# First feed-forward of a two-layer diffusion step: some lo parts of the weights by accumulating on-chip transfers, four more adaLN units on VectorE

## The chip, the cores and the metric

The kernel runs on one core of one Trainium2 chip. The time is microseconds of that core for one execution; the median of three runs counts. Profile times are microseconds from the start of the profiled execution's span, unless marked ns. Engines: PE is TensorE's matmul and PEld its weight load, DVE is VectorE, ACT ScalarE, POOL GpSimd, SP the engine that issues the loads.

## The reference, cut to what matters

Two token groups of 128 (context and latents) go through two layers. Every layer has a mixer and a gated feed-forward, each with a shift, a scale and a gate from the conditioning vector (adaLN):

```python
mod = jax.nn.silu(cond) @ w_ada[l] + b_ada[l]
sh1, sc1, gt1, sh2, sc2, gt2 = jnp.split(mod[:, None, :], 6, axis=-1)
h = rmsnorm(x, g_norm_mix[l]) * (1 + sc1) + sh1
...
x = x + gt1 * m
h = rmsnorm(x, g_norm_ffn[l]) * (1 + sc2) + sh2
x = x + gt2 * conv_ffn(h, w_ffn_up[l], w_ffn_conv[l], b_ffn_conv[l], w_ffn_down[l])
```

`conv_ffn` multiplies by `w_up` (2048 x 11264), convolves over three positions, multiplies the silu of one half by the other and multiplies by `w_down` (5632 x 2048). Everything is float32. Layer 0 has latent and grouped-query attention, layer 1 differential attention.

## The kernel before, in words

**Products.** A float32 product is made of three passes: each operand is split into hi, rounded to the matmul's type, and lo = raw - hi, and hi x hi, hi x lo and lo x hi are added in PSUM. Weights come as raw tiles of 1 MB (128 partitions x 16 blocks of 128; three buffers `raw`). `Weights.chunk` splits a tile in two halves of eight blocks: ScalarE casts raw to `wh`, VectorE subtracts to `wl` (`split`, L248 and L249; four buffers of each). `gemm` then runs 16 blocks (22 for `w_down`) x 3 matmuls of 128 x 256. Where `Weights.ahead` splits (the first products of a stage, pinned), `chunk` does not.

**adaLN units.** One unit (layer, j of six, quarter q) is 512 columns of `w_ada`, four tiles of 1 MB. It is made in one of two ways. On TensorE (`ROWS`): 16 matmuls of 32 x 512 in two pairs of steps, a copy, four transposes and a reduction (`sum_rows`, `ada_finish`); in the mixer of layer 1 these stand within the products. On VectorE (`FEATS`): eight multiply-and-sum instructions of 128 x 2048, two to a tile (`feature_step`, L473, out `junk`), two buffers `araw`, and a small add (L479). `RLIMIT` and `FLIMIT` are how far each list may be worked off by the end of a stage.

**What sets the order.** The program is written stage by stage; a scheduler puts each engine's instructions in order, save those marked to keep the written order (`keep_order`, `between`, the sums of `feature_step`). In a feed-forward, `pump(0, rate)` follows each product and hands out sums at `FRATE`: 0.7 after each of the 82 products of `up` past the first three pairs, 1.42 after 28 of the 32 of `down`. Whatever is left up to `FLIMIT` is done by a loop at the end of `ffn`. Behind the first feed-forward comes `modulated` for layer 1: its first three products (of `w_in_c`) run on the unnormed rows `u`; within the first, after 6 of 16 blocks, TensorE sums the squares (`stats`), VectorE and GpSimd make the factor (`rv` L219, `rr` L222), and after 13 blocks TensorE spreads it (`factor`). These products are pinned. The rows of the normed operand (L799 to L811) follow on VectorE, ScalarE and GpSimd.

**Queues.** All loads go through SP's queue in one order; GpSimd issues none.

Of the kernel before, what the change touches and what calls it, by code (L numbers as in the profile page):

```python
# [11 lines left out]
F32 = mybir.dt.float32  # L12
F32R = mybir.dt.float32r
AF = mybir.ActivationFunctionType
ALU = mybir.AluOpType
# [3 lines left out]
P = 128  # L19
# [57 lines left out]
ROWS = [(0, j, q) for q in range(4) for j in (1, 0)]  # L77
ROWS += [(0, j, q) for j in (2, 4) for q in range(4)]
ROWS += [(0, 5, 0)]
ROWS += [(1, 2, 1), (1, 2, 2), (1, 2, 3), (1, 4, 0), (1, 3, 0)]  # L80
FEATS = [(0, 5, 1), (0, 5, 2), (0, 5, 3)]
FEATS += [(1, j, q) for j in (1, 0) for q in range(4)]
FEATS += [(1, 2, 0)]
FEATS += [(1, 5, q) for q in range(4)]
DEEP = [[(0, 3, q) for q in range(4)], [(1, 4, q) for q in range(1, 4)] + [(1, 3, q) for q in range(1, 4)]]
RLIMIT = {"ab": 16, "ffn0": 17, "c": 22, "ffn1": 22}
FLIMIT = {"ab": 0, "ffn0": 12, "c": 12, "ffn1": 16}

SIDE = {"in3": 0.4, "heads": 1.6, "out0": 1.8, "c": 2.2, "outc": 2.0}
UW = NT + 2  # L90
# [4 lines left out]
def step_kernel(ctx: ExitStack, tc: tile.TileContext, A: dict):  # L95
    nc = tc.nc
    dve, act, pool, sp = nc.vector, nc.scalar, nc.gpsimd, nc.sync
# [25 lines left out]
    wpool = ctx.enter_context(tc.tile_pool(name="wpool", bufs=3))  # L123
# [8 lines left out]
    def banks(name):  # L132
        return tc.tile_pool(name=name, bufs=1, space=PSUM)
# [3 lines left out]
    def nm(s):  # L137
        uid[0] += 1
        return f"{s}_{uid[0]}"

    def T_(pl, shape, tag, dt=F32, bufs=None):
        kw = {} if bufs is None else {"bufs": bufs}
        return pl.tile(shape, dt, tag=tag, name=nm(tag), **kw)
# [39 lines left out]
    def step():  # L183
        for g in list(chains):
            if next(g, chains) is chains:
                chains.remove(g)
# [60 lines left out]
    def split(out_hi, out_lo, src, pin=lambda i: i):  # L247
        pin(act.copy(out_hi, src))  # L248
        pin(dve.tensor_tensor(out=out_lo, in0=src, in1=out_hi.bitcast(F32), op=ALU.subtract))  # L249
# [3 lines left out]
    class Weights:  # L253
# [3 lines left out]
        def __init__(self, src, nblk, per_tile, cycle=0):  # L257
            self.src, self.nblk, self.per = src, nblk, per_tile
            self.cycle = cycle
            self.at, self.blocks, self.tiles = 0, [], []  # L260
            self.half = None
            self.begun = []
            self.used = lambda: None

        def load(self, parts=1, pin=lambda i: i):
            n = self.per
            if self.cycle:
                n = min(n, self.cycle - self.at * n % (-(-self.cycle // n) * n))
            n *= self.nblk if self.per < TB else 1
            raw = T_(wpool, [P, 4, 512], "raw").rearrange("p g n -> p (g n)")  # L270
            w = n * P // parts
            for i in range(parts):
                s = slice(i * w, (i + 1) * w)
                pin(sp.dma_start(out=raw[:, s], in_=self.src[self.at, :, s]))
            self.at += 1
            return raw, n

# [26 lines left out]
        def chunk(self):  # L304
            while len(self.blocks) < self.nblk:
                if self.half:
                    self.ahead(lambda i: i)
                    continue
                raw, n = self.take()
                n0 = FINE if fine[0] else 8  # L310
                for lo in range(0, n, n0):
                    hi = min(lo + n0, n)
                    w = (hi - lo) * P
                    if lo % 8 == 0:
                        wh_ = T_(wpool, [P, 1024], "wh", F32R, bufs=4)
                        wl_ = T_(wpool, [P, 1024], "wl", F32R, bufs=4)
                    at = lo % 8 * P
                    wh, wl = wh_[:, at:at + w], wl_[:, at:at + w]
                    split(wh, wl, raw[:, lo * P:hi * P])
                    for b in range(hi - lo):  # L320
                        s = slice(b * P, (b + 1) * P)
                        self.blocks.append((wh[:, s], wl[:, s]))
                    self.tiles += [(wh_, wl_)] if lo % 8 == 0 else []
                self.used()
            out, self.blocks = self.blocks[:self.nblk], self.blocks[self.nblk:]
            return out
# [225 lines left out]
    class Feed:  # L552
# [5 lines left out]
        def add(self, home, load, key=None):  # L558
            self.items.append((home, load, key))

        def go(self):
            while self.items and self.free[self.items[0][0]]:
                home, load, key = self.items.pop(0)
                self.free[home] -= 1
                self.tiles[key] = load()
# [43 lines left out]
    def pump(rows, feats=0.0, until=None, beside=True):  # L609

        until = until or RLIMIT[stage[0]]
        step()
# [9 lines left out]
        feat["due"] += feats  # L622
        while feat["due"] >= 1.0 and feat["i"] < FLIMIT[stage[0]]:
            feat["due"] -= 1.0
# [876 lines left out]
    def ffn(hx, W, ready, turn, l, st):  # L1501
# [14 lines left out]
        WD = Weights(A["w_down"][l], KQ, TB)  # L1516
        cw = ada["cw"]
        with tc.tile_pool(name=f"ffn{l}", bufs=1) as fp, banks(f"pffn{l}") as pf:
            feat["home"], feat["pool"] = fp, pf
            feat["due"] = 0.0  # L1520
            in_order = [{}, {}] + turn + [{}]
            T_(fp, [P, SHIFT // 4], "pad")
# [39 lines left out]
            def down(gs, q):  # L1562
                u, rows = None, None
                if q == NQ - 1 and l < NL - 1:
                    u = raw_tile(keep, "hx")
                    rows = raw_rows(u, l + 1, 0)
                for c in range(KD):
                    quiet = q == NQ - 1 and c >= KD - QUIET[0]
                    fine[0] = quiet
                    if q == 0:  # L1570
                        ensure(l, 5, [c // 4])
                    ps = gemm(WD.chunk(), lambda k: gs[k][:, :NT], lambda k: gs[k][:, NT:2 * NT])
                    if l == NL - 1 and q == NQ - 1 and c == KD - 1:
                        last_residual(ps, l, 1, c, st)
                    else:
                        residual(ps, l, 1, c, st if q == NQ - 1 else None)
                    if rows:
                        rows(c)
                    if l == NL - 1 and q == NQ - 1 and c in EARLY:
                        act.activation(x[:, c], x[:, c], AF.Identity, scale=C("gfin")[:, c:c + 1])  # L1580
                    pump(0, 0 if quiet else FRATE["down"])
                return u

            for q in range(NQ):
                gs = up(q)
                u = down(gs, q)
            while feat["i"] < FLIMIT[stage[0]]:
                feature_step()
# [3 lines left out]
    with banks("pab") as ppool["ada"]:  # L1592
# [11 lines left out]
        with tc.tile_pool(name="beside", bufs=1) as beside:  # L1604
            o = mixer_ab(hx, beside)
            with tc.tile_pool(name="raw", bufs=1) as rp:
# [3 lines left out]
                W = Weights(A["w_up"][0], KD, 1)  # L1610
# [5 lines left out]
    with tc.tile_pool(name="cc", bufs=1) as cp, banks("pc") as ppool["ada"]:  # L1616
# [3 lines left out]
        W = Weights(A["w_in_c"], KD, 1)  # L1620
# [160 lines left out]
```

## Time and profile before

| | us |
|---|---|
| median of 3 runs | 2307.83 (2306.47 to 2307.86) |
| the profiled execution's own time | 2307.52 |
| its span | 2305.7 |
| first feed-forward, from the first products to the last | about 430 to 1163 |
| mixer of layer 1 with its first products | about 1163 to 1600 |
| second feed-forward | about 1600 to 2293 |

How to read the rows. A row of a table by stretches gives the stretch, its length, and for each engine the busy time and the number of instructions, then the granted TensorE clock (1.00 is full), the mean busy share of the 16 DMA engines and GB/s. A row of a group gives line, engine, operation, out<-in with shapes, count, then busy us and mean ns, then idle time ahead of it and what ended it. A timeline row gives start, length (over its repeats, pipelined), engine, line, operation and count, and in brackets idle time and its releaser. A row of one line's or tile's instructions gives count and min/median/max ns. A DMA row gives count, KB each and median us from issue to landing.

### The profile page before, as it was taken

The numbers are of one execution on the slowest core, as the hardware profiler recorded it, in microseconds if no ns is written. First come the engines' busy times: TensorE is split into PE (matmuls) and PEld (weight loads), VectorE is DVE, ScalarE is ACT, GpSimd is POOL, SyncE is SP. The second block draws the span as 40 slices with busy tenths as digits, with TensorE's granted clock in tenths as the row PEclk, the third lists the DMA queues.
The fourth block names the chain that finished last, engine by engine and source line by source line (L and its number), as shares of the span: only waits on it lengthen the run. The fifth ranks groups of instructions, "written<-read, shape, count | busy, mean of one in ns | idle before, by whom it ended". The sixth has DMA issues, their size and how long they took to land.

```text
span 2305.7 us, 47484 instructions
## 1 busy us (share of the span) xinstructions
PE 2275.9 (99%) x19496; PEld 2182.1 (95%) x19496; DVE 1885.6 (82%) x2973; ACT 1195.7 (52%) x1959; POOL 188.1 (8%) x238
## 2 busy tenths in 40 slices
PE   8999999999999999999999999999999999999998
PEld 6788878999999999999999999999999999999998
DVE  4667979989999999999978988898899965666654
ACT  4345555665553355555575455457555434555543
POOL 0002111300000000001130001023000000000011
PEclk9999999999999999999999999999999999999999
DMA  9987888777777777777788888776667755555553
GB/s 376 367 343 293 326 311 338 288 277 264 262 255 291 291 272 260 272 258 258 288 293 293 318 322 310 267 268 229 246 256 262 264 200 189 199 191 194 198 189 126
DMA packets 100122, 617.15 MB, mean 268 GB/s; under 512 B 10752, under 2 KB 18880, under 8 KB 33344
## 3 DMA queue, kind: packets, MB, share of 16 engines
q1 hardware_dynamic: 99904, 614.11, 72.2%
q8 instruction: 153, 2.51, 0.4%
q14 instruction: 65, 0.53, 0.1%
HBM read 609.32 MB, written 4.75 MB: 266 GB/s over the span
## 4 chain that ended last, share of the span: by engine, by line
PE 93%; DVE 3%; DMA 2%; issue 1%; POOL 1%; ACT 1%; SPq 0%; DVEq 0%; ACTq 0%; POOLq 0%
PE acc L110 86%; PE ada L110 3%; PE att L110 2%; DVE wl L249 1%; DVE hx L525 1%; DMA more<-w_ada 1%; PE att L113 1%; DMA raw<-w_out_c 0%; PE misc L110 0%; DMA araw<-w_ada 0%; DMA kvb<-w_ada 0%; POOL dev L807 0%; PE ada L113 0%; DVE rope L858 0%; ACT wh L248 0%
## 5 line engine op out<-in xcount | busy, mean ns | idle before, releaser
L110 PE MATMUL acc<-hx,wh 128*128 128x256 f32 (+1 forms) x7264 | 1255.2, 278 | 4.2 <-ACT wh L248 1.7
L248 ACT CAST wh<-raw 128x1024 fp32r<-128x1024 f32 (+1 forms) x834 | 796.6, 967 | 869.8 <-PE acc L110 736.6
L249 DVE TENSOR_TENSOR wl<-raw,wh 128x1024 fp32r<-128x1024 f32 (+1 forms) x834 | 925.4, 1126 | 246.9 <-ACT wh L248 240.2
L110 PEld LDWEIGHTS acc<-hx,wh 128*128 128x128 f32 x7264 | 1099.8, 188 | 23.2 <-ACT wh L248 8.1
L110 PE MATMUL acc<-hx,wl 128*128 128x256 f32 (+1 forms) x3632 | 1007.8, 278 | 5.3 <-DVE wl L249 5.1
L110 PEld LDWEIGHTS acc<-hx,wl 128*128 128x128 f32 x3632 | 684.5, 188 | 9.5 <-DVE wl L249 6.9
L110 PE MATMUL acc<-g,wh 128*128 128x256 f32 x2816 | 478.8, 276 | 0.0
L110 PEld LDWEIGHTS acc<-g,wh 128*128 128x128 f32 x2816 | 424.0, 188 | 0.0
L110 PE MATMUL acc<-g,wl 128*128 128x256 f32 x1408 | 388.1, 276 | 0.0
L473 DVE CUSTOM_DVE_ANT_0 junk<-araw,condb 128x2048 f32<-128x2048 f32 x128 | 294.4, 2300 | 0.0
L110 PEld LDWEIGHTS acc<-g,wl 128*128 128x128 f32 x1408 | 264.2, 188 | 0.0
L211 POOL TENSOR_TENSOR sqacc<-sqacc,sq 128x256 f32<-128x256 f32 x62 | 71.5, 1154 | 1491.1 <-ACT sq L207 1490.9
L110 PE MATMUL acc<-hxc,wh 128*128 128x256 f32 (+1 forms) x1056 | 189.3, 281 | 0.0
L110 PEld LDWEIGHTS acc<-hxc,wh 128*128 128x128 f32 x1056 | 161.9, 188 | 1.8 <-issue 1.7
L110 PE MATMUL acc<-hxc,wl 128*128 128x256 f32 (+1 forms) x528 | 146.9, 278 | 0.0
L110 PEld LDWEIGHTS acc<-hxc,wl 128*128 128x128 f32 x528 | 99.6, 189 | 0.2
L110 PE MATMUL acc<-wh,hxc 128*128 128x256 f32 (+1 forms) x512 | 95.0, 283 | 0.5 <-DVE nt L818 0.5
L1531 ACT ACTIVATE cv<-acc,convw 128x256 f32<-128x256 f32 x169 | 94.1, 557 | 0.0
L525 DVE CUSTOM_DVE_ANT_0 hx<-block,condb 128x1024 fp32r<-128x1024 f32 x65 | 79.3, 1221 | 7.3 <-DMA block<-w_ada 6.8
L1537 DVE SCALAR_TENSOR_TENSOR cv<-acc,convw,cv 128x254 f32<-128x254 f32 x169 | 81.1, 480 | 3.2
L843 DVE SCALAR_TENSOR_TENSOR x<-acc,mod,x 128x128 f32<-128x128 f32 x190 | 57.3, 344 | 31.6 <-PE acc L110 31.6
L110 PEld LDWEIGHTS acc<-wh,hxc 128*128 128x128 f32 x512 | 79.4, 188 | 3.4 <-issue 2.5
(263 smaller groups left out, 1800.4 us busy)
## 6 DMA issues: line engine op xcount, KB each, us to landing
raw<-w_up SPq DMA_DIRECT2D x176, 1024.0 KB, 4.8
araw<-w_ada SPq DMA_DIRECT2D x136, 1024.0 KB, 6.0
raw<-w_down SPq DMA_DIRECT2D x88, 1024.0 KB, 4.8
raw<-w_in_c SPq DMA_DIRECT2D x48, 1024.0 KB, 6.9
block<-w_ada SPq DMA_DIRECT2D x41, 512.0 KB, 6.8
raw<-w_in_ab SPq DMA_DIRECT2D x18, 1024.0 KB, 9.1
raw<-w_out_ab SPq DMA_DIRECT2D x16, 1024.0 KB, 7.9
raw<-w_out_c SPq DMA_DIRECT2D x16, 1024.0 KB, 7.1
```

The source lines that it names most:

```text
L110: return self.placed(nc.tensor.matmul(*a, **kw))
L113: return self.placed(nc.tensor.transpose(*a, **kw))
L211: eng.tensor_tensor(out=st["acc"], in0=st["acc"], in1=sq, op=ALU.add)
L248: pin(act.copy(out_hi, src))
L249: pin(dve.tensor_tensor(out=out_lo, in0=src, in1=out_hi.bitcast(F32), op=ALU.subtract))
L473: keep_order(dve.tensor_tensor_reduce(out=T_(feat["pool"], [P, D], "junk"), in1=feat["row"][:, c], in0=feat["raw"].rearrange("p g n -> p ( ...
L525: keep_order(dve.tensor_tensor_reduce(out=self.junk, in0=self.raw, in1=self.row[:, c].rearrange("p (g n) -> p g n", g=2), scale=1.0, scala ...
L843: dve.scalar_tensor_tensor(out=x[:, c, s], in0=ps[:, s], scalar=mod[:, l, 3 * which + 2, c, g:g + 1], in1=x[:, c, s], op0=ALU.mult, op1=AL ...
L1531: pin(act.activation(y, ps, AF.Identity, scale=cw[:, 1, m:m + 1], bias=cw[:, 3, m:m + 1]))
L1537: pin(dve.scalar_tensor_tensor(out=y3[:, :, :T - 1], in0=p3[:, :, 1:], scalar=cw[:, 2, m:m + 1], in1=y3[:, :, :T - 1], op0=ALU.mult, op1=A ...
```

## The change

It does two things. Within the first feed-forward (`W.far` and `WD.far` are set for layer 0), the second half of every odd tile gets its lo part another way: ScalarE casts raw to `wh` and writes `-wh` into a buffer `far` (two buffers, in place of `wl`), and a transfer issued by GpSimd adds the raw half, 512 KB, onto it on chip. Halves that are split in finer steps (the last columns of the stage), or by `ahead`, stay as they were; the built program holds 61 such transfers. Second, four units, (1,2,1), (1,2,2), (1,2,3) and (1,4,0), move from `ROWS` to `FEATS`. The limits follow: VectorE has to have 16 units done by the end of the first feed-forward instead of 12, and TensorE's list ends at 18 instead of 22. `FRATE` stays.

```diff
-ROWS += [(1, 2, 1), (1, 2, 2), (1, 2, 3), (1, 4, 0), (1, 3, 0)]
+ROWS += [(1, 3, 0)]
 FEATS = [(0, 5, 1), (0, 5, 2), (0, 5, 3)]
 FEATS += [(1, j, q) for j in (1, 0) for q in range(4)]
-FEATS += [(1, 2, 0)]
+FEATS += [(1, 2, q) for q in range(4)] + [(1, 4, 0)]
 FEATS += [(1, 5, q) for q in range(4)]
...
-RLIMIT = {"ab": 16, "ffn0": 17, "c": 22, "ffn1": 22}
-FLIMIT = {"ab": 0, "ffn0": 12, "c": 12, "ffn1": 16}
+RLIMIT = {"ab": 16, "ffn0": 17, "c": 18, "ffn1": 18}
+FLIMIT = {"ab": 0, "ffn0": 16, "c": 16, "ffn1": 20}
...
+            self.src_of.append((raw, self.at))
...
+                    i = next(i for r, i in self.src_of if r is raw)
+                    far = self.far and lo == 8 and n0 == 8 and i % 2
...
-                        wl_ = T_(wpool, [P, 1024], "wl", F32R, bufs=4)
+                        wl_ = T_(self.far, [P, 1024], "far", F32R, bufs=2) if far else T_(wpool, [P, 1024], "wl", F32R, bufs=4)
...
-                    split(wh, wl, raw[:, lo * P:hi * P])
+                    if far:
+                        act.copy(wh, raw[:, lo * P:hi * P])
+                        act.activation(wl, wh.bitcast(F32), AF.Copy, scale=-1.0)
+                        pool.dma_start(out=wl, in_=raw[:, lo * P:hi * P], accum_op=ALU.add)
+                    else:
+                        split(wh, wl, raw[:, lo * P:hi * P])
...
+            if l == 0:
+                W.far = WD.far = fp
```

The line numbers grow by 9 to 11: L473 becomes L482, L479 L488, L702 L711, L843 L852, L1531 L1542.

Three places of the order follow. First VectorE at the end of the first feed-forward, before (x is the residual row, hx the unnormed operand, wl of raw_14225 and later are of `w_in_c`):

```order
L249 TENSOR_TENSOR wl_14303<-raw_14300,wh_14302 128x512 x2
L843 SCALAR_TENSOR_TENSOR x_76<-acc_14129,mod_77,x_76 128x128 x2
L249 TENSOR_TENSOR wl_14309<-raw_14300,wh_14308 128x512 x2
L702 SCALAR_TENSOR_TENSOR hx_12699<-x_76,scl_78,hx_12699 128x128 x2
L219 TENSOR_SCALAR rv_14264<-att_14259 128x2
L249 TENSOR_TENSOR wl_14379<-raw_14376,wh_14378 128x512 x2
```

The same place of the changed program:

```order
L852 SCALAR_TENSOR_TENSOR x_76<-acc_14194,mod_77,x_76 128x128 x2
L249 TENSOR_TENSOR wl_14471<-raw_14462,wh_14470 128x512 x2
L711 SCALAR_TENSOR_TENSOR hx_12752<-x_76,scl_78,hx_12752 128x128 x2
L482 ISA junk_14269,mod_77<-araw_13892,condb_5747 128x2048
...
L482 ISA junk_14362,mod_77<-araw_14358,condb_5747 128x2048
L482 ISA mod_77 128x1
L488 TENSOR_TENSOR mod_77<-mod_77,cst_74 128x8
L463 SCALAR_TENSOR_TENSOR scl_78<-mod_77,cst_74 128x8
L219 TENSOR_SCALAR rv_14426<-att_14421 128x2
L249 TENSOR_TENSOR wl_14541<-raw_14538,wh_14540 128x512 x2
```

Between hx and rv, where nothing stood, there are 31 sums now, each with its read of the accumulator; the third weight tile's lo part is still behind rv.

Second, ScalarE at one odd tile of the up projection (raw_6628 before, raw_6635 after; cv is a convolution step of an earlier product), before:

```order
L248 CAST wh_6630<-raw_6628 128x1024
L1553 ACTIVATE cv_6482<-cv_6482 128x256
L248 CAST wh_6634<-raw_6628 128x1024
L1531 ACTIVATE cv_6549<-acc_6500,convw_2384 128x256
L248 CAST wh_6698<-raw_6696 128x1024
```

and now:

```order
L248 CAST wh_6637<-raw_6635 128x1024
L1564 ACTIVATE cv_6488<-cv_6488 128x256
L324 CAST wh_6641<-raw_6635 128x1024
L1542 ACTIVATE cv_6556<-acc_6507,convw_2384 128x256
L248 CAST wh_6706<-raw_6704 128x1024
L325 ACTIVATE far_6642<-wh_6641 128x1024
```

The negation far_6642 stands behind a convolution step and the next tile's cast. 13 of the 61 stand behind such a cast.

Third, TensorE at the same half now (acc_6714 is the next tile's product):

```order
L110 MATMUL acc_6646<-hx_5342,wh_6641 128x256 x2
L110 MATMUL acc_6714<-hx_5342,wh_6706 128x256 x2
L110 MATMUL acc_6714<-hx_5342,wl_6707 128x256
...
L110 MATMUL acc_6646<-hx_5342,far_6642 128x256
```

Between the first two hi matmuls of the half and the first that reads far_6642 there are 21 matmuls of the next tile; before, lo followed hi directly.

More of the change, by code (lines that the diff above doesn't have):

```diff
@@ L263, in __init__ @@
             self.used = lambda: None
+            self.far, self.src_of = None, []
         def load(self, parts=1, pin=lambda i: i):
```

## The prediction, made before the run

> **What bounds the kernel now.** I read the page's head and the chain of waits first, then a table by stretches of the first feed-forward and of the mixer behind it, then the groups of VectorE and ScalarE in that feed-forward.
>
> ```profile
> span 2305.7 us, 47484 instructions
> ...
> PE 2275.9 (99%) x19496; PEld 2182.1 (95%) x19496; DVE 1885.6 (82%) x2973; ACT 1195.7 (52%) x1959; POOL 188.1 (8%) x238
> ...
> PE 93%; DVE 3%; DMA 2%; issue 1%; POOL 1%; ACT 1%; SPq 0%; DVEq 0%; ACTq 0%; POOLq 0%
> ```
>
> The chain is TensorE. A stretch in which TensorE waits is added to the span, a matmul that goes is taken off it, and work taken from another engine is worth nothing unless TensorE was waiting for it. The table by stretches says where it waits:
>
> ```profile
> 430.00:660.00 230.00, 230.00 (x2019) 226.86 (x2018) 208.75 (x303) 136.65 (x217) 18.94 (x27) 1.00 0.72 263
> ...
> 760.00:1000.00 240.00, 240.00 (x2120) 240.00 (x2120) 222.47 (x283) 120.48 (x158) 0.00 (x0) 1.00 0.74 270
> ...
> sum 735.00, PE 735.00 PEld 731.86 DVE 680.38 ACT 387.99 POOL 36.49; mean PE 183.75 PEld 182.96 DVE 170.10 ACT 97.00 POOL 9.12
> ...
> 1190.00:1520.00 330.00, 328.46 (x2752) 312.82 (x2752) 287.94 (x498) 172.33 (x325) 26.59 (x36) 1.00 0.83 303
> ```
>
> The sum line is the first feed-forward, 430 to 1165 us: TensorE is busy for 735.00 of 735 us, so VectorE's 680.38 are all hidden there, and relief of VectorE alone buys nothing. The last row is the differential mixer: TensorE 328.46 of 330.
>
> **What the change takes away.** In the first feed-forward these are the groups it touches:
>
> ```profile
> L249 DVE TENSOR_TENSOR wl<-raw,wh 128x1024 fp32r<-128x1024 f32 x244 | 296.1, 1235 | 38.0 <-ACT wh L248 36.7
> L473 DVE CUSTOM_DVE_ANT_0 junk<-araw,condb 128x2048 f32<-128x2048 f32 x96 | 221.0, 2302 | 0.0
> ...
> L248 ACT CAST wh<-raw 128x1024 fp32r<-128x1024 f32 x244 | 256.8, 1054 | 307.0 <-PE acc L110 267.5 <-ACT g L248 31.4 <-issue 6.4
> L1531 ACT ACTIVATE cv<-acc,convw 128x256 f32<-128x256 f32 x85 | 47.3, 557 | 0.0
> ```
>
> The built program holds 61 accumulating transfers (42 for the up projection, 19 for the down), so 61 subtractions of 1.235 us leave VectorE: 75 us, worth 0 by the sum line above. ScalarE gets 61 negations, which I price as its cast of the same shape, 1.054: 64 us on an engine that is busy 388 of 735. Hidden too, save as latency, below.
>
> The four units leave TensorE in the mixer. What one cost there:
>
> ```profile
> 1244.38 0.28 PE L110 MATMUL acc<-hxc,wh 128*128 128x256 f32 x1
> 1244.59 1.92 PE L110 MATMUL ada<-araw,condw 128*32 128x512 f32 x16
> 1246.44 0.38 PE L110 MATMUL acc<-hxc,wh 128*128 128x256 f32 x1
> ...
> 1291.00 0.28 PE L110 MATMUL acc<-hxc,wh 128*128 128x256 f32 x1
> 1291.11 0.60 PE L113 MATMUL ada<-cst,am 128*128 128x128 f32 x4
> 1291.47 0.36 PE L110 MATMUL acc<-hxc,wh 128*128 128x256 f32 x1
> ...
> L110 PE MATMUL ada<-araw,condw x128: 592/592/617, 1244.6 to 1505.3; 128*32 128x512 f32 x128
> ```
>
> A pair of sums pushes the next product matmul from 0.12 us behind the last to 2.06, so it costs 1.94; the four turns of a unit cost 0.47 - 0.12 = 0.35. The last row counts 128 records after 1190 us, eight pairs of 16, which is four units: 8 x 1.94 + 4 x 0.35 = **16.9 us off the path**. (The one unit still on TensorE is summed ahead of 1190 us.) Ends: 14, if a few of these gaps hid other waits, and 18. The casts, reductions and adds that go with the units were hidden and count 0, as do 16 loads of 1 MB that leave this stage.
>
> **Where the four units land.** The rates at which a feed-forward hands sums to VectorE are not changed. They placed 96 sums before (the row x96: twelve units of eight) and place 97 now, but the limit is 128. So 31 sums are left to the loop at the end of the feed-forward, and the order shows them on VectorE as one block between the last row of the mixer's operand (L702 before) and the statistic rv (L219). What stands at that place today:
>
> ```profile
> 1164.85 0.61 DVE L702 SCALAR_TENSOR_TENSOR hx<-x,scl,hx 128x128 fp32r<-128x128 f32 x2
> ...
> 1166.10 0.16 DVE L219 TENSOR_SCALAR rv<-att 128x2 f32<-128x2 f32 x1 [0.64 <-PE att L110]
> 1166.34 0.70 POOL L222 TENSOR_TENSOR rr<-rv,cst 128x2 f32<-128x2 f32 x1 [7.55 <-DVE rv L219]
> ...
> 1168.40 0.28 PE L110 MATMUL acc<-hx,wh 128*128 128x258 f32 x1
> 1168.52 0.60 PE L110 MATMUL att<-cst,rr 128*128 128x128 f32 x4
> ```
>
> TensorE needs rr at 1168.5, within the first product of the next stage. Its order is fixed there (the product's hooks are pinned), so everything behind waits: the rest of that product, and the second one, whose lo parts were made before the block. Queued behind the block on VectorE are rv, the lo parts of the third weight tile and all rows of the new operand. Nothing else is left for TensorE. The length of the block:
>
> ```profile
> 1137.22 2.29 DVE L473 CUSTOM_DVE_ANT_0 junk<-araw,condb 128x2048 f32<-128x2048 f32 x1
> 1139.43 0.14 DVE L473 DVE_READ_ACCUMULATOR2_ANT mod<- 128x1 f32 x1
> ...
> 1148.57 0.75 DVE L479 TENSOR_TENSOR mod<-mod,cst 128x8 f32<-128x8 f32 x1
> ...
> DMA to landing us min/median/max: 4.7/5.0/8.5
> ```
>
> A sum holds VectorE 2.21 us (1137.22 to 1139.43), at most 2.35 with its read behind it: 31 make 69 to 73, and five small adds at up to 0.75 make it 70 to 77. The 15 tiles still to load could pace it instead: two buffers, 5.0 to land (the last row, the loads of these tiles in this feed-forward) and 4.5 to use give (5.0 + 4.5) / 2 = 4.75 a tile, with the first half tile 73. I take 74. The block then runs from 1165.5 to 1239.5, rv and rr take until 1240.5, and TensorE, which would have gone on at 1168.4, has lost **72 us** (67 to 77). I add 1 for the row unit's tiles, whose loads now queue behind the block's on SP, and 2 for the clock, which this trace shows cut early in the run:
>
> ```profile
> 15.00:20.00 5.00, 5.00 (x38) 3.38 (x41) 0.16 (x1) 0.37 (x1) 0.70 (x1) 0.59 1.00 419
> ```
>
> At 0.59 for 5 us, 2 us are lost; bounds 0 and 4. The Trainium skill, "TensorE: Matmul & The Clock Gate" (The HAM clock gate), states that an idle window cuts the clock and that about 3.4 us of work restore it, which would cost some 2 us by its figures; by that rule the trace agrees in kind.
>
> **The transfers.** Each lo part now goes cast, negation on ScalarE, issue on GpSimd, transfer, matmul. Two rows say how early it starts:
>
> ```profile
> 703.48 1.06 ACT L248 CAST wh<-raw 128x1024 fp32r<-128x1024 f32 x1 [1.89 <-PE acc L110]
> 706.20 1.06 ACT L248 CAST wh<-raw 128x1024 fp32r<-128x1024 f32 x1 [1.66 <-PE acc L110]
> ```
>
> A cast waits for TensorE to leave a hi buffer; halves are 2.72 us apart (24 matmuls of 0.113), and with four buffers TensorE reaches the new half three halves later and its lo part two matmuls on: 8.4 us. Cast and negation take 2.1, hand-overs 0.2: 6.1 are left for the transfer. In 13 of 61 the next tile's cast stands between cast and negation and waits a half longer, which leaves 3.4; in some 25 a convolution step of 0.557 does. Against that the scheduler has put up to 38 matmuls of the next tile ahead of late ones. For the half in the order quoted above, 72 + 2 + 21 matmuls make 10.7 us, less 2.72, 2.1 and 0.2: 5.7. Going through the order in this way, 15 of the 61 have 2.1 to 4.4 us, 27 have 5.1 to 6.0 and 19 have 6.1 to 9.6. Summing what is short, TensorE waits 2 us in all if a transfer takes 3.5, 19 at 5.0, 37 at 5.7, 97 at 7, 154 at 8, 220 at 9.1.
>
> No transfer of GpSimd and none that adds is in the trace. The nearest rows:
>
> ```profile
> raw<-w_up SPq DMA_DIRECT2D x176, 1024.0 KB, 4.8
> ...
> raw<-w_in_c SPq DMA_DIRECT2D x48, 1024.0 KB, 6.9
> raw<-w_in_ab SPq DMA_DIRECT2D x18, 1024.0 KB, 9.1
> ...
> o_y<-x SPq DMA_DIRECT2D x3, 384.0 KB, 2.7
> ...
> L274 SPq DMA_DIRECT2D raw<-w_up x45: 327/328/328, 659.8 to 1018.4; - x45
> ```
>
> Low end 3.5: 512 KB between the 384 KB of o_y (2.7) and the 1 MB of w_up (4.8) would be 3.1, and an issue as long as SP's, 0.33. High end 9.1: 1 MB in the busiest stage. An add has to read both its operands, 1 MB for 512 KB written, so the nearest row is w_up, 4.8 us in this very stage; with that issue on top, and with the queues fuller than now, I take 5.7: **37 us**. The queues hold it: 0.74 busy at 270 GB/s, and 61 x 1 MB more in 735 us is 87 GB/s, so about 0.98 at most. The raw tile is held some 6 us longer, but its next load lands 5 us after that, about when its cast is wanted.
>
> The Trainium skill, "DMA: Bandwidth & Descriptors" (Anatomy of one DMA), fits 2.0 us plus bytes at 436 GB/s, and "Collectives: The Full Stack" (The bandwidth ceiling) says that a reduction reads two sources: an estimate of 4.4 us, by which this term would be about 10 and the sum 2376. No run shows it yet.
>
> **Sum.** 2305.7 + 72 + 1 + 2 - 16.9 + 37 = 2400.8 us of span; the profiled execution took 2307.5 around a span of 2305.7, and the median of the runs shown is 2307.8, so 2 on top: **2403 us**.
>
> **Rivals.** (a) The transfers are in time: 4 us or less, at most 8 us of waits; only block and units count, 2307.5 + 75 - 17 + 4 = 2370. For it: VectorE and GpSimd are free of much of their work; against it: the w_up row. (b) The transfers come late nearly every time, 7 us and more: 2366 + 97 to 220, so 2463 to 2586. For it: up to 0.98 of the queues, and a path through GpSimd that nobody has timed. A mechanism that gives it: GpSimd's issue waits for a VectorE instruction to end, up to 2.3 us by the L473 row, which makes 5.7 into 8.0 and costs 154: 2520. The Trainium skill, "SBUF — State Buffer" (Who interferes with whom), has such a lock for some VectorE modes, but infers that a tensor_tensor, VectorE's main work here, spares descriptor writing. (c) The other side: the block is hidden. It pays from the point where TensorE loses less than the 16.9 us gained; since only 3 us of its work stand ahead of rr, the block would have to be under 19 us, 0.6 per sum against 2.21 measured. Then the transfers must be in time too: 2307.5 - 16.9 = 2291. Against it stands the order itself. (d) The change doesn't do all it says: 61 transfers instead of the number named is in the count already.
>
> **How the numbers follow.** Forecast 2403 with waits of 10 to 90 us: 0.50. (a) 0.24, (b) 0.23, (c) and a draw 0.03. The range goes from the bottom of (a), 2307.5 + 68 - 18 + 1 = 2358, to 7.5 us per transfer (waits of 125), 2491; so 2357 to 2492, which leaves out (c) and the upper part of (b), under 0.2. A change of 0.2% is what measurements of this kernel can tell from none: slower 0.965, faster 0.02, same 0.015.
>
> **What would show it.** Right: a VectorE stretch of some 74 us of L482 alone near the end of the first feed-forward, with TensorE idle for about 72 and waiting for rr; ada records after it down by 128; TensorE waiting for far tiles in the feed-forward for some 37 us, and DMA share there near 0.9. Wrong: transfers landing in under 4 us or over 7, by far the largest unknown; or TensorE idle for well under 67 us at the stage's end, by which the block would be broken up.

## The result, and the profile after

The changed kernel takes 2511.57 us (median of four runs, 2506.28 to 2517.66) against 2307.15 for the kernel before: ratio 1.0889, 95% interval 1.0862 to 1.0917. The forecast of 2403 us had the direction right and 109 us too little; the range ended at 2492. All times here and below are of executions at the usual granted clock; one execution of the last experiment, 2809.51 us at 0.759 of the clock, is left out. The profiled execution took 2517.66 us around a span of 2515.9, 210.2 us more than the span before.

The head of the page of the changed kernel and its chain of waits:

```profile
span 2515.9 us, 47397 instructions
...
PE 2320.4 (92%) x19352; PEld 2230.5 (89%) x19352; DVE 1898.2 (75%) x2972; ACT 1250.4 (50%) x2016; POOL 242.8 (10%) x299
...
PE 64%; DMA 14%; issue 12%; DVE 7%; ACT 2%; POOL 1%; SPq 0%; POOLq 0%; DVEq 0%; ACTq 0%
```

TensorE was 93% of the chain and is 64% now; transfers are 14%. Its busy time rose by 44.5 us although it has 144 matmuls less, so it also works more slowly somewhere. The timelines of TensorE and VectorE at the end of the first feed-forward cut the run into three pieces (start, length, then the instruction, in brackets what it waited for):

```profile
1312.07 2.29 DVE L482 CUSTOM_DVE_ANT_0 junk<-araw,condb 128x2048 f32<-128x2048 f32 x1
...
1384.86 2.30 DVE L482 CUSTOM_DVE_ANT_0 junk<-araw,condb 128x2048 f32<-128x2048 f32 x1
...
1387.36 0.56 PE L110 MATMUL att<-cst,sqacc 128*128 128x1 f32 x2 [75.37 <-DVE mod L482]
...
1389.23 0.16 DVE L219 TENSOR_SCALAR rv<-att 128x2 f32<-128x2 f32 x1 [1.61 <-PE att L110]
```

In the timeline of the kernel before, the statistics' matmul stood here:

```profile
1165.11 0.28 PE L110 MATMUL att<-cst,sqacc 128*128 128x1 f32 x2
```

Now TensorE reaches it at 1311.99 and starts it at 1387.36. So the feed-forward grew by 146.9 us, the block took 75.4, and from there to the end it is 1128.5 instead of 1140.6: 12.1 less. Together 210.2.

Where the 146.9 come from is told by the waits of TensorE from 430 to 1312 us (in total, times, longest):

```profile
PE acc L110 <- DMA far<-raw: 76.9, 35, 6.2
PE acc L110 <- ACT wh L248: 7.4, 4, 5.3
PE acc L110 <- DVE cv L1548: 2.6, 4, 1.2
PE acc L110 <- DVE wl L249: 1.2, 2, 0.8
```

and by the table by stretches, first the whole feed-forward, then one wait of 4.22 us for a transfer and what follows it:

```profile
430.00:1312.00 882.00, 793.97 (x6469) 781.04 (x6467) 622.32 (x856) 442.53 (x627) 86.16 (x101) 0.96 0.79 261
...
691.50:695.87 4.37, 0.16 (x2) 0.00 (x0) 2.68 (x4) 0.42 (x1) 0.00 (x0) 0.85 0.71 158
695.87:701.37 5.50, 5.50 (x25) 5.50 (x26) 0.00 (x0) 0.61 (x1) 0.00 (x0) 0.50 0.81 298
701.40:704.10 2.70, 2.70 (x24) 2.70 (x24) 1.39 (x3) 2.70 (x4) 0.47 (x1) 1.00 0.41 173
```

Waits make 88.1 us, 76.9 of them for transfers. The other 59 are matmuls that take longer: busy time was 735.00 before and is 793.97. Part of that is the clock. After the wait it is granted at 0.50 for 5.50 us, in which 25 matmuls go where 49 would have gone; by the starts of the matmuls there are 14 such stretches, and these cost some 26 us. Most of the remaining 33 us has two sources. The first is a slower pace: between the waits, at a granted clock of 1.00, matmuls often start every 0.118 us instead of every 0.113. By the starts, that is by each interval between two matmuls against 0.113 us, that makes 17 us (3741 intervals); at 0.005 us each, all 6469 matmuls of the feed-forward could lose no more than about 30. The runs below take this up. The second is the edge of each wait. A matmul's record runs 0.28 us from start to end, while the next one normally starts after 0.113, and the first interval behind a wait is longer by another 0.11; so a wait costs some 0.28 us on top of its listed length, 12 us for 45.

The transfers (durations min/median/max in ns, first and last start; then us from issue to landing):

```profile
L326 POOL DMA_DIRECT2D far<-raw x61: 855/865/1089, 471.8 to 1267.6; - x61
...
DMA to landing us min/median/max: 4.5/6.6/10.9
```

They land after 6.6 us, where 5.7 was taken. The matmuls of TensorE's units are 128 fewer, as read from the rows of `ada` (608 before):

```profile
L110 PE MATMUL ada<-araw,condw x480: 376/592/1062, 13.1 to 1409.4; 128*32 128x512 f32 x138, 128*32 128x256 f32 x22
```

### The profile page after: what moved, and what is told of

It is laid out like the page before. It is cut to its first block, busy times and chain, and to the rows that moved or that the text cites. A ratio compares the mean times of both kernels' runs of the same rounds, so it can differ in the third digit from the quotient of the medians.

```text
span 2515.9 us, 47397 instructions
## 1 busy us (share of the span) xinstructions
PE 2320.4 (92%) x19352; PEld 2230.5 (89%) x19352; DVE 1898.2 (75%) x2972; ACT 1250.4 (50%) x2016; POOL 242.8 (10%) x299
## 4 chain that ended last, share of the span: by engine, by line
PE 64%; DMA 14%; issue 12%; DVE 7%; ACT 2%; POOL 1%; SPq 0%; POOLq 0%; DVEq 0%; ACTq 0%
PE acc L110 59%; DMA far<-raw 6%; DMA raw<-w_up 5%; DVE junk L482 3%; PE ada L110 2%; DMA raw<-w_down 2%; PE att L110 2%; DVE wl L249 2%; DMA araw<-w_ada 1%; DMA kvb<-w_ada 1%; ACT wh L248 1%; DVE hx L534 1%; DMA block<-w_ada 0%; PE att L113 0%; PE misc L110 0%
## 5 line engine op out<-in xcount | busy, mean ns | idle before, releaser
L248 ACT CAST wh<-raw 128x1024 fp32r<-128x1024 f32 (+2 forms) x773 | 732.4, 960 | 805.7 <-PE acc L110 580.9
L249 DVE TENSOR_TENSOR wl<-raw,wh 128x1024 fp32r<-128x1024 f32 (+2 forms) x773 | 852.0, 1115 | 307.5 <-ACT wh L248 303.8
L110 PE MATMUL acc<-hx,wl 128*128 128x256 f32 (+1 forms) x3296 | 918.8, 279 | 5.6 <-DVE wl L249 5.4
L110 PEld LDWEIGHTS acc<-hx,wl 128*128 128x128 f32 x3296 | 623.0, 189 | 9.0 <-DVE wl L249 7.2
L482 DVE CUSTOM_DVE_ANT_0 junk<-araw,condb 128x2048 f32<-128x2048 f32 x160 | 366.8, 2293 | 1.8 <-DMA araw<-w_ada 0.3
L110 PE MATMUL acc<-g,wl 128*128 128x256 f32 x1256 | 345.9, 278 | 1.2 <-DVE wl L249 1.2
L324 ACT CAST wh<-raw 128x1024 fp32r<-128x1024 f32 x61 | 64.3, 1054 | 224.4 <-PE acc L110 224.4
L110 PE MATMUL acc<-hx,far 128*128 128x256 f32 x336 | 104.3, 310 | 50.3 <-DMA far<-raw 50.3
L326 POOL DMA_DIRECT2D far<-raw x61 | 52.9, 868 | 705.6 <-ACT far L325 468.5
L110 PEld LDWEIGHTS acc<-hx,far 128*128 128x128 f32 x336 | 70.0, 208 | 55.5 <-DMA far<-raw 55.3
L852 DVE SCALAR_TENSOR_TENSOR x<-acc,mod,x 128x128 f32<-128x128 f32 x190 | 57.4, 344 | 52.5 <-PE acc L110 52.4
```

The source lines that it names most:

```text
L110: return self.placed(nc.tensor.matmul(*a, **kw))
L324: act.copy(wh, raw[:, lo * P:hi * P])
L326: pool.dma_start(out=wl, in_=raw[:, lo * P:hi * P], accum_op=ALU.add)
L482: keep_order(dve.tensor_tensor_reduce(out=T_(feat["pool"], [P, D], "junk"), in1=feat["row"][:, c], in0=feat["raw"].rearrange("p g n -> p ( ...
L852: dve.scalar_tensor_tensor(out=x[:, c, s], in0=ps[:, s], scalar=mod[:, l, 3 * which + 2, c, g:g + 1], in1=x[:, c, s], op0=ALU.mult, op1=AL ...
```

## The experiments

Times are medians; ratios are to the kernel before on the same chip, with 95% intervals. In the diffs, + and - are against the changed kernel, or against the run that is named.

**The units alone.**

```diff
-            if l == 0:
-                W.far = WD.far = fp
```

> The four units on VectorE alone, with the changed limits and unchanged rates; every lo part is a subtraction again, no transfer is issued. Theory (the block and the transfers are two separate losses): the first feed-forward ends where it ended before, then VectorE works off some 31 sums in about 75 us with TensorE idle, and the mixer is 17 us shorter: 2307 + 75 - 17 + 2, so about 2367 us (2358 to 2376). Rival (the block costs more than its sums, because loads of the unit tiles and of the next weights queue behind each other): over 2385.

2366.47 us, ratio 1.0268 (1.0251 to 1.0285). TensorE's waits show the same block alone:

```profile
PE att L110 <- DVE mod L482: 75.5, 1, 75.5
```

The time is within the expected range: the block and the units' gain come without any transfer, at about the predicted size. In this feed-forward TensorE is busy 720.00 of 720 us up to 1150 and its pace is 0.113.

**The transfers alone**: `ROWS`, `FEATS`, `RLIMIT` and `FLIMIT` put back, `far` kept.

> The 61 accumulating transfers alone; units, limits and rates as before the change. Theory: the first feed-forward grows as it did in the changed kernel, from 735 to about 882 us, of which some 88 are waits of TensorE, 26 half clock behind such waits and 30 a slower pace of the matmuls: 2307 + 146 = 2453 us (2430 to 2470). Rival (the prediction's 37 us of waits was right for the transfers, and the surplus came from the 16 more unit tiles): about 2345.

2447.22 us, 1.0617 (1.0597 to 1.0637): 142 us more than before, within the expected range. The pace of 0.118 makes 19 us of it by the starts, not the 30 that were expected. Waits for the transfers, and their landing:

```profile
PE acc L110 <- DMA far<-raw: 72.6, 33, 6.9
...
DMA to landing us min/median/max: 4.5/6.2/11.2
```

With the units' 61 the two parts make 203 us, and the whole change made 204: they add up, and the surplus over the forecast is the transfers' alone.

**Both, without the block.**

```diff
-FRATE = {"up": 0.7, "down": 1.42}
+FRATE = {"up": 0.925, "down": 1.88}
```

> The changed kernel with the rates raised by 1.32 (0.925 and 1.88), so that the 128 sums are handed out within the feed-forward and none is left for a block. Theory (losses add up): the block's 75 us go, the transfers' 146 stay: 2511 - 75 = 2436 us (2420 to 2450). Rival (the block only hid work that VectorE has no room for): the sums delay convolution steps and lo parts instead, and no more than 40 us are gained: over 2470.

2442.9 us (2422.8 to 2447.2), 1.0567 (1.051 to 1.0623), as expected: 69 us less than the changed kernel, so the block was the rates' fault. Of the units' 17 us only about 4 show against the transfers alone, within the scatter.

**Transfers that nobody reads.** Against the transfers alone, behind the transfer:

```diff
+                        wl = T_(wpool, [P, 1024], "wl", F32R, bufs=4)[:, :w]
+                        dve.tensor_tensor(out=wl, in0=raw[:, lo * P:hi * P], in1=wh.bitcast(F32), op=ALU.subtract)
```

> As with the transfers alone, but nobody reads their result: cast, negation, issue and transfer run as in the changed kernel, and VectorE makes the lo part that TensorE reads by its subtraction as before. The 61 transfers are work for nothing here. Theory (the loss is latency, TensorE waiting for the result): TensorE waits for no transfer, pace 0.113 us a matmul as before, 2307 to 2322 us, the upper end from raw tiles that are held longer. Rival (the loss is traffic or GpSimd's issue, whoever waits): the slower pace of 0.118 us a matmul stays and costs 30 us or more: 2335 to 2400.

2378.63 us, 1.0319 (1.029 to 1.0348): the rival's time, but neither one's picture. TensorE waits for no transfer, and yet half of the loss stays. ScalarE's casts wait for raw tiles, which they did not before, and the transfers land later still:

```profile
ACT wh L248 <- DMA raw<-w_up: 165.8, 61, 8.7
ACT wh L248 <- DMA raw<-w_down: 91.4, 29, 8.5
...
DMA to landing us min/median/max: 4.5/9.9/12.1
```

A raw tile can't be loaded again before the transfer has read it. TensorE's waits, for casts, lo parts and convolution steps, come to 39 us, and the pace of 0.118 is there for about half of the time, 12 us by the starts.

**A copy instead of the add** (`accum_op` left out; otherwise the transfers alone).

> As with the transfers alone, but each transfer copies the raw half over the negated one and adds nothing, so the lo parts of these halves are the raw values; bytes written, issue and order stay. Theory (the add makes the transfer long, since it reads a second operand): a copy lands in about 4 us instead of 6.2, TensorE waits under 10 us for them by the prediction's own table, and 2315 to 2350 us come out, with 10 to 30 us of slower pace. Rival (the route makes it long: GpSimd's queue and an on-chip copy beside the loads): it lands in 5.8 us or more and the time is over 2410 us.

2359.19 us, 1.0236 (1.0221 to 1.0252).

```profile
PE acc L110 <- DMA far<-raw: 11.5, 9, 2.4
...
DMA to landing us min/median/max: 2.9/4.1/8.5
```

The same route with the same bytes written lands 2.1 us earlier, so it is the add that makes the transfer late, and not the route through GpSimd. GpSimd's issue is 0.33 us of the difference (median 0.862 us for an add, 0.530 for a copy); and between 470 and 1100 us the packets of one add took 1.9 times as much of the DMA engines' time as those of one copy. That this is the add's second read is likely, but not shown. The waits are close to the expected 10 us; the time is 9 us over the theory's end, since the pace is 0.118 nearly throughout.

**Transfers in two parts.** Against the transfers alone:

```diff
-                        pool.dma_start(out=wl, in_=raw[:, lo * P:hi * P], accum_op=ALU.add)
+                        for s in (slice(0, w // 2), slice(w // 2, w)):
+                            pool.dma_start(out=wl[:, s], in_=raw[:, lo * P:hi * P][:, s], accum_op=ALU.add)
```

> As with the transfers alone, each transfer cut in two of 256 KB, 122 in all. Theory (length goes with bytes): the first part lands some 1.5 us earlier than the whole did, the second is wanted 1.4 us later by TensorE, and of 73 us of waits about 30 stay: 2380 to 2410 us. Rival (a fixed cost sets the length): both parts land after 6 us, the second 0.9 us later for GpSimd's second issue, and nothing is gained: 2440 to 2465 us.

2441.21 us, 1.0589 (1.057 to 1.0608): the rival's time, but neither one's picture. Over both parts the median is no shorter than a whole transfer's, as the rows show; but the first part landed 5.4 us after its issue, the second 7.7 (8.3 after the first one's issue), medians of 61. The first is 0.8 us earlier than a whole one and the second 2.1 later, so neither a length by bytes nor a fixed one fits:

```profile
L327 POOL DMA_DIRECT2D far<-raw x122 | 107.2, 1034 | 646.8 <-ACT far L325 408.4
...
DMA to landing us min/median/max: 3.3/6.7/12.7
```

**GpSimd subtracts**, first with units and raised rates, then alone.

```diff
-                        act.activation(wl, wh.bitcast(F32), AF.Copy, scale=-1.0)
-                        pool.dma_start(out=wl, in_=raw[:, lo * P:hi * P], accum_op=ALU.add)
+                        pool.tensor_tensor(out=wl, in0=raw[:, lo * P:hi * P], in1=wh.bitcast(F32), op=ALU.subtract)
```

> The changed kernel with the same 61 lo parts made by one subtraction on GpSimd instead of negation and transfer, and the rates raised by 1.32 so that no block is left. Theory: GpSimd needs about 4.6 us for a half (1.15 us for 128x256 in the trace), within the 7.1 us from cast to need, so TensorE waits for nothing there and the four units' 17 us are gained: 2285 to 2300 us, faster than both kernels. Rival (VectorE's own instructions grow while GpSimd works beside it, or GpSimd takes over 7 us for a half): TensorE waits for lo parts, 2330 us or more.

> GpSimd's subtraction for the 61 halves alone, units, limits and rates as before the change. Theory: TensorE loses nothing, 2305 to 2312 us. Rival: as in the run before this one, GpSimd late or VectorE slower beside it: 2330 us or more, which would be the price of the subtraction itself without the units.

2389.53 us, 1.0355 (1.031 to 1.0401), and 2337.28 us, 1.0138 (1.0123 to 1.0153): the rival's time both times. The groups of the first of the two, 430 to 1160 us:

```profile
L249 DVE TENSOR_TENSOR wl<-raw,wh 128x1024 fp32r<-128x1024 f32 x170 | 301.4, 1785 | 5.4 <-ACT wh L248 5.3
L481 DVE CUSTOM_DVE_ANT_0 junk<-araw,condb 128x2048 f32<-128x2048 f32 x113 | 280.3, 2480 | 0.1
...
L325 POOL TENSOR_TENSOR far<-raw,wh 128x1024 fp32r<-128x1024 f32 x57 | 165.3, 2899 | 514.2 <-ACT wh L324 514.2
```

GpSimd is quick enough (2.9 us), but VectorE's own subtractions go from 1.235 to 1.785 us and its sums from 2.30 to 2.48. The Trainium skill, "SBUF — State Buffer" (SBUF: two separate sides), has an exclusive lock between a GpSimd instruction that reads SBUF and a VectorE instruction with two inputs there; these rows agree. Alone, the subtraction leaves TensorE waiting for only 4 us in the feed-forward, and still costs 32: the pace is 0.118 from 506 us nearly to the end, 27 us by the starts.

**Where the slower pace comes from.** Two runs without transfers, negations or GpSimd, units as before: the 61 lo parts made by VectorE into the far buffers, and the far buffers only set aside.

```diff
                     if far:
                         act.copy(wh, raw[:, lo * P:hi * P])
-                        act.activation(wl, wh.bitcast(F32), AF.Copy, scale=-1.0)
-                        pool.dma_start(out=wl, in_=raw[:, lo * P:hi * P], accum_op=ALU.add)
+                        dve.tensor_tensor(out=wl, in0=raw[:, lo * P:hi * P], in1=wh.bitcast(F32), op=ALU.subtract)
...
-                        wl_ = T_(self.far, [P, 1024], "far", F32R, bufs=2) if far else T_(wpool, [P, 1024], "wl", F32R, bufs=4)
+                        wl_ = T_(wpool, [P, 1024], "wl", F32R, bufs=4)
+                        if far: T_(self.far, [P, 1024], "far", F32R, bufs=2)
```

(The last three lines are the second run's only.)

> The 61 lo parts are written to the two far buffers, but by VectorE's subtraction as before: no negation, no transfer, no GpSimd, and the instructions of every engine stand in the order of the kernel before, but for two. Theory (the slower pace of 0.118 us a matmul comes from where the lo part lies): the pace is 0.118 in most of the feed-forward without a wait, and 2325 to 2340 us come out. Rival (it comes from transfers, GpSimd's work, or the changed order of matmuls): 0.113, 2304 to 2310 us.

> As in the run before this one, but the two far buffers are only set aside and never used; the lo part goes to the four wl buffers in turn. Theory (which lo buffer goes with which hi buffer matters; here the two turn in step again): 2304 to 2310 us. Rival (the two buffers push the other tiles of the feed-forward's pool to other places, and that makes the pace slower): 2325 to 2340 us.

2332.56 us, 1.0116 (1.0103 to 1.013), and 2304.91 us, 0.9996 (0.9987 to 1.0005). The same stretch of the two, by count of matmuls:

```profile
600.00:1000.00 400.00, 400.00 (x3399) 400.00 (x3398) 358.66 (x446) 185.69 (x239) 0.00 (x0) 1.00 0.71 263
```

```profile
600.00:1000.00 400.00, 400.00 (x3532) 400.00 (x3531) 369.86 (x465) 196.15 (x251) 0.00 (x0) 1.00 0.74 271
```

Both are what the theory expected. TensorE is busy throughout at full granted clock in both, and does 4% fewer matmuls in the first. Writing the lo part of every fourth half to another buffer is enough for that: 27 us, with no instruction added.

**Transfers into the wl buffers**, no far buffers (against the transfers alone):

```diff
-                        wl_ = T_(self.far, [P, 1024], "far", F32R, bufs=2) if far else T_(wpool, [P, 1024], "wl", F32R, bufs=4)
+                        wl_ = T_(wpool, [P, 1024], "wl", F32R, bufs=4)
```

> The transfers alone, but they add onto the four wl buffers, and no far buffers are set aside. Theory (place and latency are two separate losses): TensorE waits for transfers as long as with far buffers, about 73 us, with half clock behind the waits, but the pace is 0.113 between: 2415 to 2435 us. Rival (the slower pace follows waits or transfers): 2440 to 2455 us.

2447.01 us, 1.0608 (1.059 to 1.0625): the expectation missed. The pace is 0.113 for most of the time here, as expected, but the waits grew to 84 us from 81 (all releasers, 430 to 1300 us) with more half clock behind them. By the starts the pace costs 11 us less than with far buffers, half clock 8 us more and the waits 3.5 more, so the sum is the same. That a faster TensorE only reaches the late transfers sooner is a likely reason, not a tested one.

**GpSimd's subtraction into the wl buffers**, by the same edit:

> GpSimd's subtraction for the 61 halves, units and limits as before the change, written into the four wl buffers instead of far buffers. Theory (of the 30 us that GpSimd's subtraction cost, the slower pace of TensorE was nearly all, and it came with the far buffers): 2305 to 2314 us. Rival (GpSimd's work itself makes TensorE's pace slower, or VectorE late): 2325 to 2340 us.

2333.14 us, 1.012 (1.0106 to 1.0134): a miss too. The pace is 0.118 from 561 to 1134 us without any far buffer; it set in behind a wait of 1.02 us for VectorE. So the far buffers are one way into the slower pace and not its cause.

**Two units, then one, with raised rates and no transfers.** Against the units alone, for two units (one unit likewise, rates 0.755 and 1.53; `RLIMIT` and `FLIMIT` follow):

```diff
-FRATE = {"up": 0.7, "down": 1.42}
+FRATE = {"up": 0.81, "down": 1.64}
...
-ROWS += [(1, 3, 0)]
+ROWS += [(1, 2, 3), (1, 4, 0), (1, 3, 0)]
...
-FEATS += [(1, 2, q) for q in range(4)] + [(1, 4, 0)]
+FEATS += [(1, 2, q) for q in range(3)]
...
```

> No transfers; two of the four units, (1,2,1) and (1,2,2), on VectorE, limits accordingly, rates raised by 1.15, so that the 112 sums are handed out and no block is left. Theory: VectorE has 55 us left in the first feed-forward and needs 16 x 2.3 = 37, so nothing waits and half of the units' gain shows: 2305 - 8.4 = 2297 us (2294 to 2301). Rival (at 717 of 735 us VectorE is late with lo parts here and there, and half clock follows each wait of TensorE): 2306 us or more.

> No transfers; one unit, (1,2,1), on VectorE, the other three stay on TensorE; rates raised by 1.08 for 104 sums, none left for a block. Theory (VectorE has the room, and the miss with two units came from one bubble of 0.27 us behind which TensorE kept the slower pace): without such a bubble 2305.5 - 4.2, so 2299 to 2303 us. Rival (any further sum disturbs TensorE's order enough for the slower pace): 2306 us or more.

Two units: 2311.57 us, 1.0031 (1.002 to 1.0041), the rival's time. TensorE never waits in the feed-forward; but its timeline has one gap in the starts, 0.38 us where 0.11 is usual, and the pace on either side of it differs:

```profile
845.56 0.28 PE L110 MATMUL acc<-hx,wl 128*128 128x256 f32 x1
845.94 0.47 PE L110 MATMUL acc<-hx,wh 128*128 128x256 f32 x2
```

```profile
600.00:840.00 240.00, 240.00 (x2120) 240.00 (x2119) 230.94 (x281) 109.75 (x132) 0.00 (x0) 1.00 0.77 288
850.00:1090.00 240.00, 240.00 (x2040) 240.00 (x2039) 224.49 (x295) 122.04 (x175) 5.03 (x3) 1.00 0.72 263
```

4% of the 310 us that follow are 12 us, all but 3 of the distance between the expected 2297 and the result. With one unit the pace stays 0.113, and 2303.08 us come out, as expected: 0.999 (0.9981 to 0.9999), well below the changed kernel, but too close to the kernel before to be safely told from it. What made the gap with two units was not tried.

**An earlier start of the chain.** Against the transfers alone, hi buffers of their own for the 61 halves; then, in addition, the transfer's source in HBM instead of the raw tile.

```diff
-                        wh_ = T_(wpool, [P, 1024], "wh", F32R, bufs=4)
+                        wh_ = T_(self.far, [P, 1024], "own", F32R, bufs=2) if far else T_(wpool, [P, 1024], "wh", F32R, bufs=4)
...
-                        pool.dma_start(out=wl, in_=raw[:, lo * P:hi * P], accum_op=ALU.add)
+                        pool.dma_start(out=wl, in_=self.src[i, :, lo * P:hi * P], accum_op=ALU.add)
```

(The last two lines are the second run's only.)

> The transfers alone, but the hi parts of the 61 halves get two buffers of their own, so that their cast need not wait for TensorE to leave one of the four others; everything else as with the transfers alone. Theory (the loss is lead: the chain of cast, negation, issue and transfer starts too late): the cast starts up to two halves, 5.4 us, earlier, a landing of 6.2 us is in time, TensorE waits under 20 us for transfers and 2330 to 2370 us come out, the slower pace of some 25 us remaining. Rival (the loss is traffic: earlier issues only land later, as the unread transfers did with 9.9 us, or raw tiles that are held longer make the casts late): over 2400 us.

> As with own hi buffers, but the transfer takes the raw half from the weight in HBM instead of from the raw tile on chip (a second read of the same numbers), so a raw tile is free as soon as ScalarE and VectorE have read it. Theory (with the earlier start, what is left is the raw tile held until the transfer has landed, which makes later loads and casts late): the casts' 267 us of waits for raw tiles shrink to under 60, TensorE's waits of 46 us to under 20, and 2340 to 2375 us come out, 25 to 30 of it the slower pace. Rival (traffic: transfers land after 8.6 us because the queues are shared with the loads, wherever the source lies): 2400 us or more.

2411.31 us, 1.0464 (1.0448 to 1.048), and 2402.30 us, 1.0409 (1.0388 to 1.043). With own buffers:

```profile
PE acc L110 <- DMA far<-raw: 31.6, 20, 3.7
...
ACT own L324 <- DMA raw<-w_up: 158.3, 40, 7.6
...
DMA to landing us min/median/max: 4.6/8.6/13.8
```

The waits for transfers fell from 72.6 to 31.6, though transfers that start earlier land after 8.6 us. With the source in HBM 10 us are left in three waits, and the transfers land after 5.6 us, but other waits take their place:

```profile
PE acc L110 <- DVE cv L1548: 15.5, 14, 1.6
PE acc L110 <- ACT g L248: 12.2, 2, 6.7
PE acc L110 <- DVE wl L249: 10.3, 21, 0.8
PE acc L110 <- DMA far<-w_up: 7.1, 2, 6.2
...
ACT own L324 <- DMA raw<-w_up: 155.2, 36, 6.1
```

ScalarE still stands before casts whose raw tile has not landed, with convolution steps and the casts of `g` queued behind them; TensorE waits for those. Neither expectation held whole. The times are the rivals', over 2400 us. The earlier start takes most of the transfers' own waits away, as the first theory had it, though waits of all kinds still make some 50 us; and holding the raw tile was not what was left, since the casts wait for raw tiles as long with the source in HBM. Traffic is not ruled out as the reason: the loads of `w_up` landed after 4.9 us before the change, 6.7 with the transfers alone and 8.0 here (470 to 1100 us).

## Why the prediction was wrong, point by point

**The transfers' waits.** The step that failed is "with that issue on top, and with the queues fuller than now, I take 5.7: 37 us". Within it the size was off: 6.6 us were measured. The prediction's own table, between 37 us at 5.7 and 97 at 7, gives 79 at 6.6, and the waits for transfers were 76.9. So the counting of leads was about right, but part of the agreement is luck: for the transfers alone the table gives 60 at 6.2, and 72.6 were measured. What the term had too small is the price of adding: an add lands 2.1 us behind a copy of the same bytes beside the same loads.

**The raw tile.** The prediction took its longer hold as harmless, since the next load would land "about when its cast is wanted". That step was wrong too: with transfers that nobody reads, ScalarE's casts waited 257 us for raw tiles, and TensorE stood for 39 us. How much of that is the hold and how much the traffic stays open.

**What a wait costs besides itself.** This term was left out, and it is the larger miss. The sum charged half clock once, 2 us behind the block, and took a wait of TensorE at its length. The feed-forward had 45 waits and 14 stretches at half clock: 26 us. The pace of 0.118 took 17 us, the edges of the waits some 12, and 11 went to waits for casts, lo parts and convolution steps; a few us stay unaccounted for. 37 forecast, 147 measured: 40 from the size, 70 from what was not in the sum.

**The block**: 75.4 us against 72, since each sum took 2.40 us with its read (the upper end that was given, 2.35). The place was wrong: TensorE stood already at the first matmul of the statistics, 6 blocks into the product, and not at the factor behind 13. The program itself holds a wait there, on VectorE's count, until the last sum's read; it stands in the traces of the two kernels with a block, and in neither the kernel before nor the one with raised rates. The places of the order quoted before the run do not show TensorE here; which tile asks for the wait was not tried.

**The units**: from the statistics to the end 12.1 us less, where -16.9 + 1 + 2 = -13.9 was summed. The granted clock of 0.72 in the 12.7 us behind the block costs 3.5 where 2 was taken, which nearly closes the gap. Right.

**The rivals.** (b) has the time, 2463 to 2586, but for another reason: the transfers took 6.6 us at the median, not 7 or more, and its mechanism does not show: GpSimd's issue took 0.855 to 1.089 us on all 61, without a wait of 2.3, and a copy by the same path landed in 4.1. (c) fell with the block. DMA share was to be near 0.9 and was 0.79: the stage became longer. The range was too narrow because its upper end priced only the waits themselves.

## What to carry to other kernels

Where TensorE is the bound and never waits, price a wait at more than its length: here 77 us of waits for transfers came with 59 us of longer matmul time and 11 us of further waits. Relief of an engine that TensorE does not wait for could not show here, while the longer chain behind a hi buffer that is freed late had a price although each link is cheap: with hi buffers of their own the waits for transfers fell from 72.6 to 31.6 us. Work that is added to a list must be added to the rates that hand it out, or it comes as a block: 69 us here.

## What the runs showed of the hardware

- TensorE has two paces at a granted clock of 1.00: 0.113 and 0.118 us a matmul. It changes between them behind waits, behind a bubble of 0.27 us, or with another lo buffer, and then stays for tens to hundreds of us. With two units every weight load took 187 or 188 ns ahead of the bubble, and behind it every third took 192. What sets the pace is open.
- The granted clock goes by a fixed grid. In the trace of the changed kernel it changes only at multiples of 3.413 us counted from 1.67 us. Over the nine runs with transfers, 92 grid windows between 430 and 1312 us were followed by a cut to 0.50, each after TensorE had stood for at least 1.66 us of the window, and every full-clock window in which it stood for more than 1.94 us was followed by one. So it took about half a window without work, where the prediction spoke of an idle window. Full clock came back behind a window with at most 0.52 us of standing. In the rows below the time without work is the length less PE's busy time. A wait of 1.78 us that lies in one window costs clock in the next; one of 3.35 us that the grid splits does not:

```profile
612.66:616.07 3.41, 1.63 (x15) 1.44 (x14) 2.29 (x3) 0.93 (x2) 0.00 (x0) 1.00 0.94 318
616.07:619.48 3.41, 3.41 (x19) 3.41 (x18) 0.00 (x0) 0.44 (x1) 0.00 (x0) 0.50 0.87 346
...
1032.50:1035.91 3.41, 1.80 (x16) 1.60 (x14) 3.38 (x7) 1.78 (x3) 0.00 (x0) 1.00 1.01 304
1035.91:1039.32 3.41, 1.67 (x13) 1.67 (x14) 2.72 (x3) 0.00 (x0) 0.00 (x0) 1.00 0.50 102
1039.32:1042.73 3.41, 3.41 (x32) 3.41 (x31) 0.64 (x2) 2.22 (x3) 0.00 (x0) 1.00 0.96 401
```

  The Trainium skill, "TensorE: Matmul & The Clock Gate" (The HAM clock gate), has a free-running window of about 3.4 us in which activity is judged; by that rule it matters where in the window a wait falls, and these rows agree with it.
- Transfers of 512 KB from issue to landing beside the loads, medians of a run: a copy on chip 4.1 us, an add on chip 6.2 to 6.6, and 8.6 to 9.9 where it starts earlier or nobody reads it; an add with its source in HBM 5.6; two adds of 256 KB in a row 5.4 and 7.7.
- GpSimd's subtraction slows VectorE: with the 61 taken off it (and units as before), VectorE was busy 1907.6 us where it had been 1885.6.
